# Moving the low halves of 38 weight slabs from VectorE to GpSimd around the norms of a two-layer hybrid backbone

## The chip, the cores and the metric

The kernel runs on one core of a Trainium2 chip. The metric is the device time of one execution in microseconds (us); a kernel's time is the median of its runs. Engines: PE (TensorE, matmul), DVE (VectorE), ACT (ScalarE), POOL (GpSimd), and SP, whose queue issues the DMAs here.

## What is computed

Two layers over 256 context and 256 latent tokens of width 1024. Each layer is a half-step feed-forward, a mixer with three branches on one input projection, and another half-step feed-forward, all between RMS norms:

```python
def ffn_sublayer(x, mod, pre_w, post_w, w_i, w_o):
    shift, scale, gate = mod
    h = modulate(rms_norm(x, pre_w), shift, scale)
    return x + 0.5 * gate * rms_norm(swiglu(h, w_i, w_o), post_w)
...
        u_lat = modulate(rms_norm(h_lat, nw[2]), m_lat[3], m_lat[4])
        p_lat = jnp.split(u_lat @ w_in[l], split_pts, axis=-1)
...
        h_lat = h_lat + m_lat[5] * rms_norm(y_lat, nw[3])
        h_lat = ffn_sublayer(h_lat, m_lat[6:9], nw[4], nw[5], ffn_w_in[l, 1], ffn_w_out[l, 1])
```

The context stream does the same until the second layer's mixer; only the latent stream is returned.

## The kernel before, in words

Activations lie feature-major: 8 tiles of 128 features by 512 tokens (context in columns 0 to 255, stream 0; latents in 256 to 511, stream 1). Every f32 product is made of three matmuls over a high and a low part of each side (`mm3`, lines 206 to 208: high by high, high by low, low by high). A weight slab is 128 x 1024 f32, one DMA of 512 KB. It is split on arrival:

```python
        raw = self.wr_p.tile(shape, F32, name="raw", tag="raw")
        nc.sync.dma_start(raw, src)
        hi = self.wh_p.tile(shape, F32R, name="whi", tag="whi")
        lo = self.wl_p.tile(shape, F32R, name="wlo", tag="wlo")
        nc.scalar.copy(hi, raw)
        (eng or nc.vector).tensor_tensor(lo, raw, hi.bitcast(F32), ALU.subtract)
```

`raw` has 3 buffers, `whi` and `wlo` 4 each. ACT makes `whi` (L200); `wlo = raw - whi` (L201) is DVE's, unless `eng` says otherwise or `self.share` gives every third slab to POOL, as it does during the latent attention and the merge beside it.

Where one sublayer ends and the next begins the two token streams are staggered. `out_phase` runs the last 8 output tiles stream by stream (`by_stream`), and after each stream's tiles calls `norms`: a post-norm of the output `y`, the addition to the residual `h`, the next pre-norm, and its modulation into `uh` and `ul`, the input of the next matmuls. While one stream is in `norms`, PE works on the other. The next sublayer begins the same way: its first tiles (three pairs of feed-forward tiles, `FRONT`, or five projection tiles) also go stream by stream, stream 0 while stream 1 is still in its norms. Call such a place a handoff. There are five: 1, first feed-forward of layer 0 to its projection; 2, output projection of the mixer to the second feed-forward; 3, that to layer 1's first feed-forward; 4, that to layer 1's projection; 5, layer 1's output projection to the last feed-forward, with the latent stream alone.

The links of a norm, by line: ACT squares (`sq`, L280); POOL, for the post-norm, adds seven squares (`sqa`, L284); PE sums them over features (`ssum`, L295); DVE makes the reciprocal root in ten small operations on 128x2 (`rv` L259 to the last `ry` L271, "the root chain"); PE spreads it (`pbc`, L678); then for each of 8 tiles DVE makes `pn` (L329), DVE or POOL adds it to `h` (L330, five of eight on POOL), and after the second root chain DVE makes `u` (L314), ACT `uh` (L316) and DVE `ul` (L317). In handoffs 1, 3 and 4 DVE also adds each output tile to `y` (L502) before it is squared. `pn`, `u` and the `y` addition have one input in PSUM; `ul`, `wlo` and the additions to `h` have both in SBUF.

The order of the instructions on each engine is set by a list scheduler when the program is built; engines run their queues in order.

Of the kernel before, what the change touches and what calls it, by code (L numbers as in the profile page):

```python
# [21 lines left out]
NK = 8  # L22
# [15 lines left out]
NFIRST = 4  # L38
# [95 lines left out]
class K:  # L134
# [56 lines left out]
    def slab(self, src, shape, eng=None):  # L191
        nc = self.nc
        if eng is None and self.share:
            self.nslab += 1
            eng = nc.gpsimd if self.nslab % self.share == 0 else None
# [6 lines that stand above are left out]
        return hi, lo  # L202
# [233 lines left out]
    def ffn(self, l, f, streams=(0, 1), skew=SKEW, ada=(), after=None, start=False):  # L436

        tc, nc = self.tc, self.nc
        n = 0 if f == 0 else 4
        s0 = 0 if f == 0 else 6  # L440
        full = slice(HALF[streams[0]][0], HALF[streams[-1]][1])
        halves = [slice(*HALF[c]) for c in streams]
        split = len(streams) > 1
        with ExitStack() as es:
            ad = es.enter_context(self.pool(name=f"ad{l}{f}", bufs=1))
            pre = self.start(ad, None) if start else None
            if ada and not start:
                self.silu_rows(ad)
            fp = self.fp = es.enter_context(self.pool(name=f"ffn{l}{f}", bufs=1))
            gen = self.ada_gen(ada)  # L450
            due, per = 0.0, (len(ada) * NK + 2) / (60 - (4 if start else 0))

            def step(w):
                nonlocal due
                due += per * w
                while due >= 1:
                    due -= 1
                    next(gen, 0)

            y = [fp.tile([128, T], F32, name=f"y{m}") for m in range(NK)]  # L460
            for g, (f0, f1) in enumerate(FG):
                last = g == len(FG) - 1
                acts = []
                j = f0
                while j < f1:
                    grp = list(range(j, j + (2 if pre and j == 0 else FRONT if j == 0 and split else 1)))
                    at = {jj: (fp.tile([128, T], F32R, name="ah", tag="ah", bufs=10),
                               fp.tile([128, T], F32R, name="al", tag="al", bufs=10)) for jj in grp}
                    slab = lambda jj: [self.slab(self.A["fin"][l, f, jj, q], [128, NK, 128]) for q in range(2)]
                    if pre and j == 0:  # L470
                        for jj in grp:
                            self.ffn_in(full, at[jj], pre[jj], True)
                    elif len(grp) > 1:
                        self.by_stream(grp, streams, slab, lambda jj, c, sl: self.ffn_in(halves[c], at[jj], sl))
                    else:
                        self.ffn_in(full, at[j], slab(j))
                    acts += [at[jj] for jj in grp]
                    j += len(grp)
                    if not (pre and j <= 2):
                        step(2 * len(grp))  # L480
                if last:
                    for _ in gen:
                        pass
                    gain = self.mod_scale(l, s0 + 2, n + 1, 0.0, 0.5, f"fga{l}{f}")
                nk = f1 - f0

                def oslab(m):
                    return self.slab(self.A["fout"][l, f, m][:, f0:f1, :], [128, nk, 128])

                def out_tile(ms, cols, s):  # L490
                    (m,), (s,) = ms, s
                    if not last:
                        step(1)
                    wh, wl = s
                    ps = self.acc.tile([128, T], F32, name="fo", tag="acc")
                    for k in range(nk):
                        ah, al = acts[k]
                        self.mm3(ps[:, cols], wh[:, k, :], wl[:, k, :], ah[:, cols], al[:, cols], k == 0, k == nk - 1)
                    if g == 0:
                        nc.scalar.copy(y[m][:, cols], ps[:, cols])  # L500
                    else:
                        nc.vector.tensor_tensor(y[m][:, cols], y[m][:, cols], ps[:, cols], ALU.add)  # L502

                self.y = y
                self.out_phase(out_tile, oslab, streams, full, skew if last and split else 0, gain if last else None, after)
# [190 lines left out]
    def gdn_pre(self, l, last, ph, pb):  # L696

        nc, A, gp = self.nc, self.A, self.gp
# [16 lines left out]

        nv = max(0, NFIRST - 4)
        vtm = [pb.tile([128, 4, 128], F32, name="vtm", tag="vtm", bufs=4) for _ in range(nv)]
        self.by_stream([21] + list(range(NFIRST)), (0, 1), lambda i: self.win_slab(l, i), half)
        self.mkr = self.dram.tile([64, T], F32, name=f"mkr{l}")
        nc.sync.dma_start(self.mkr, kr[0:64])  # L720
        ps = kr[64:80]
# [39 lines left out]
        for h in range(4):  # L761
            q = ph.tile([128, T - q0], F32, name="qT", tag="qT", bufs=4)
# [909 lines left out]
```

## Time and profile before

| what | value |
|---|---|
| median of 3 runs | 2602.57 us (2599.68 to 2602.64) |
| the profiled execution | 2603.4 us, of which the span of its instructions 2601.6 us |
| PE busy | 2517.8 us (97%) |
| DVE busy | 1763.1 us (68%) |
| ACT busy | 1056.1 us (41%) |
| POOL busy | 261.5 us (10%) |
| mean granted PE clock | 0.981 of full speed |

Busy is time in which an engine executes; a DVE or POOL instruction that has begun and is held up counts as busy, so a mean duration above the shortest ones tells of holding up. The windows view gives busy time and the clock of a stretch, the timeline an engine's instructions in order with the idle time before each in brackets and what ended it.

### The profile page before, as it was taken

The numbers are of one execution on the slowest core, as the hardware profiler recorded it, in microseconds if no ns is written. First come the engines' busy times: TensorE is split into PE (matmuls) and PEld (weight loads), VectorE is DVE, ScalarE is ACT, GpSimd is POOL, SyncE is SP. The second block draws the span as 40 slices with busy tenths as digits, with TensorE's granted clock in tenths as the row PEclk, the third lists the DMA queues.
The fourth block names the chain that finished last, engine by engine and source line by source line (L and its number), as shares of the span: only waits on it lengthen the run. The fifth ranks groups of instructions, "written<-read, shape, count | busy, mean of one in ns | idle before, by whom it ended". The sixth has DMA issues, their size and how long they took to land.

```text
span 2601.6 us, 42990 instructions
## 1 busy us (share of the span) xinstructions
PE 2517.8 (97%) x17034; PEld 2202.6 (85%) x17034; DVE 1763.1 (68%) x3364; ACT 1056.1 (41%) x1742; POOL 261.5 (10%) x248
## 2 busy tenths in 40 slices
PE   7999999999999999999999999999999899998998
PEld 5888888888888877998888898888989798788998
DVE  6778668674787454685665687767678678755554
ACT  3432235545444343553222443223465444554543
POOL 0000012012100012400000200000302110023001
PEclk9999999999999999999999999999999899998999
DMA  7556543234232331565444456555334325334653
GB/s 266 179 194 197 170 142 123 98 107 133 74 135 87 110 104 57 170 195 169 151 142 144 140 169 201 177 174 162 115 108 125 124 91 199 122 114 139 189 185 122
DMA packets 121561, 377.37 MB, mean 145 GB/s; under 512 B 14736, under 2 KB 24208, under 8 KB 121360
## 3 DMA queue, kind: packets, MB, share of 16 engines
q1 hardware_dynamic: 121360, 374.63, 45.2%
q8 instruction: 134, 2.20, 0.3%
q14 instruction: 67, 0.55, 0.1%
HBM read 352.69 MB, written 21.89 MB: 144 GB/s over the span
## 4 chain that ended last, share of the span: by engine, by line
PE 85%; DVE 7%; ACT 3%; issue 2%; DMA 2%; POOL 1%; SPq 0%; POOLq 0%; ACTq 0%; DVEq 0%
PE fgu L206 11%; PE fgu L208 11%; PE fgu L207 11%; PE pj L206 7%; PE pj L208 7%; PE pj L207 7%; PE fo L207 5%; PE fo L208 5%; PE fo L206 5%; DVE wlo L201 1%; PE pbc L678 1%; PE ssum L295 1%; PE br L206 1%; PE br L207 1%; PE br L208 1%
## 5 line engine op out<-in xcount | busy, mean ns | idle before, releaser
L200 ACT CAST whi<-raw 128x1024 fp32r<-128x1024 f32 (+1 forms) x486 | 500.9, 1032 | 977.9 <-issue 305.1
L201 DVE TENSOR_TENSOR wlo<-raw,whi 128x1024 fp32r<-128x1024 f32 (+1 forms) x460 | 559.3, 1217 | 267.9 <-ACT whi L200 259.7
L206 PE MATMUL fgu<-uh,whi 128*128 128x512 f32 (+1 forms) x1504 | 529.6, 354 | 2.7 <-ACT uh L316 2.2
L207 PE MATMUL fgu<-ul,whi 128*128 128x512 f32 (+1 forms) x1504 | 529.7, 353 | 0.1
L208 PE MATMUL fgu<-uh,wlo 128*128 128x512 f32 (+1 forms) x1504 | 529.5, 353 | 0.2 <-DVE wlo L201 0.2
L206 PE MATMUL pj<-uh,whi 128*128 128x512 f32 (+1 forms) x1072 | 381.3, 357 | 8.6 <-ACT whi L200 4.4
L208 PE MATMUL pj<-uh,wlo 128*128 128x512 f32 (+1 forms) x1072 | 375.5, 353 | 1.9 <-POOL wlo L201 1.2
L207 PE MATMUL pj<-ul,whi 128*128 128x512 f32 (+1 forms) x1072 | 376.2, 352 | 0.0
L231 DVE CUSTOM_DVE_ANT_0 junk<-wa,cb,bada 128x1024 f32<-128x1024 f32 x268 | 343.5, 1282 | 11.6 <-DMA wa<-in_ada 7.0
L206 PEld LDWEIGHTS fgu<-uh,whi 128*128 128x128 f32 x1504 | 286.5, 191 | 41.7 <-ACT uh L316 3.1
L208 PEld LDWEIGHTS fgu<-uh,wlo 128*128 128x128 f32 x1504 | 286.6, 191 | 38.6 <-DVE wlo L201 1.0
L207 PEld LDWEIGHTS fgu<-ul,whi 128*128 128x128 f32 x1504 | 286.7, 191 | 37.9 <-DVE ul L317 0.5
L207 PE MATMUL fo<-al,whi 128*128 128x256 f32 (+1 forms) x896 | 291.4, 325 | 0.5 <-DVE al L434 0.3
L208 PE MATMUL fo<-ah,wlo 128*128 128x256 f32 (+1 forms) x896 | 290.6, 325 | 0.0
L206 PE MATMUL fo<-ah,whi 128*128 128x256 f32 (+1 forms) x896 | 290.5, 325 | 0.0
L206 PEld LDWEIGHTS pj<-uh,whi 128*128 128x128 f32 x1072 | 208.9, 195 | 31.5 <-ACT whi L200 4.7
L208 PEld LDWEIGHTS pj<-uh,wlo 128*128 128x128 f32 x1072 | 208.5, 195 | 25.2 <-POOL wlo L201 1.9
L207 PEld LDWEIGHTS pj<-ul,whi 128*128 128x128 f32 x1072 | 209.2, 195 | 21.0 <-DVE ul L317 0.4
L284 POOL TENSOR_TENSOR sqa<-sqa,sq 128x256 f32<-128x256 f32 x60 | 63.5, 1058 | 1297.7 <-ACT sq L280 1295.9
L207 PEld LDWEIGHTS fo<-al,whi 128*128 128x128 f32 x896 | 168.7, 188 | 17.0 <-DVE al L434 1.6
L206 PEld LDWEIGHTS fo<-ah,whi 128*128 128x128 f32 x896 | 168.5, 188 | 15.3
L208 PEld LDWEIGHTS fo<-ah,wlo 128*128 128x128 f32 x896 | 168.5, 188 | 15.3
(368 smaller groups left out, 3497.5 us busy)
## 6 DMA issues: line engine op xcount, KB each, us to landing
raw<-in_fin SPq DMA_DIRECT2D x184, 512.0 KB, 3.5
wa<-in_ada SPq DMA_DIRECT2D x136, 512.0 KB, 4.1
raw<-in_win SPq DMA_DIRECT2D x128, 512.0 KB, 3.5
raw<-in_fout SPq DMA_DIRECT2D x79, 512.0 KB, 3.6
raw<-in_fout SPq DMA_DIRECT2D x32, 384.0 KB, 3.2
raw<-in_wb SPq DMA_DIRECT2D x24, 512.0 KB, 3.6
raw<-in_wo SPq DMA_DIRECT2D x21, 512.0 KB, 3.8
ws<-in_ada SPq DMA_DIRECT2D x8, 512.0 KB, 7.9
```

Of the source, the lines that this page charges most:

```text
L200: nc.scalar.copy(hi, raw)
L201: (eng or nc.vector).tensor_tensor(lo, raw, hi.bitcast(F32), ALU.subtract)
L206: nc.tensor.matmul(out, wh, xh, start=start, stop=False)
L207: nc.tensor.matmul(out, wh, xl, start=False, stop=False)
L208: nc.tensor.matmul(out, wl, xh, start=False, stop=stop)
L231: op = nc.vector.tensor_tensor_reduce(out=self.junk, in0=w, in1=self.cb[:, t], scale=1.0, scalar=self.bada[:, l, i, m:m + 1], op0=ALU.mult ...
L284: eng.tensor_tensor(S["acc"], S["acc"], sq, ALU.add)
L295: nc.tensor.matmul(S["ps"][:, i:i + 1], a[:, i * 128:(i + 1) * 128], self.ones[:, 0:1], start=S["first"], stop=(m == NK - 1 and a is S["pa ...
L678: self.nc.tensor.transpose(pb[:, c * 128:(c + 1) * 128], y[:, c:c + 1].to_broadcast([128, 128]), self.ident)
```

## The change

`slab` gets an engine at two places: POOL for the first three pairs of feed-forward tiles where there are two streams, for the first two tiles of the last feed-forward, and for the five projection tiles that go stream by stream. Slabs that are loaded a second time for stream 1 are included: 7 slabs in handoffs 1 and 4, 10 in handoffs 2 and 3, 4 in handoff 5, 38 in all. The slabs of the output tiles in the same handoffs stay on DVE.

```diff
@@ -466,7 +466,9 @@
+
+                    eng = nc.gpsimd if len(grp) > 1 or (f == 1 and not split and j < 2) else None
-                    slab = lambda jj: [self.slab(self.A["fin"][l, f, jj, q], [128, NK, 128]) for q in range(2)]
+                    slab = lambda jj: [self.slab(self.A["fin"][l, f, jj, q], [128, NK, 128], eng) for q in range(2)]
@@ -715,7 +717,8 @@
-        self.by_stream([21] + list(range(NFIRST)), (0, 1), lambda i: self.win_slab(l, i), half)
+
+        self.by_stream([21] + list(range(NFIRST)), (0, 1), lambda i: self.win_slab(l, i, nc.gpsimd), half)
```

The scheduler then orders the queues anew. Line numbers from L467 on are 2 or 3 higher in the changed kernel.

POOL's queue in handoff 1, from the square sums of stream 1's output to its last addition to the residual, before:

```order
L284 TENSOR_TENSOR sqa<-sqa,sq 128x256 x6
L330 TENSOR_TENSOR h_103<-h_103,pn 128x256
L330 TENSOR_TENSOR h_104<-h_104,pn 128x256
L330 TENSOR_TENSOR h_106<-h_106,pn 128x256
L330 TENSOR_TENSOR h_107<-h_107,pn 128x256
L330 TENSOR_TENSOR h_109<-h_109,pn 128x256
```

and in the changed kernel:

```order
L284 TENSOR_TENSOR sqa<-sqa,sq 128x256 x4
L201 TENSOR_TENSOR wlo<-raw,whi 128x1024 x4
L284 TENSOR_TENSOR sqa<-sqa,sq 128x256 x2
L201 TENSOR_TENSOR wlo<-raw,whi 128x1024
L330 TENSOR_TENSOR h_103<-h_103,pn 128x256
L330 TENSOR_TENSOR h_104<-h_104,pn 128x256
L201 TENSOR_TENSOR wlo<-raw,whi 128x1024
L330 TENSOR_TENSOR h_106<-h_106,pn 128x256
L330 TENSOR_TENSOR h_107<-h_107,pn 128x256
L330 TENSOR_TENSOR h_109<-h_109,pn 128x256
```

Four slabs now stand ahead of the last two square sums, one ahead of the additions to `h` and one among them. Handoffs 3 and 4 read the same at this place; in handoff 2 it is two, then three, and five behind the additions.

DVE's queue in handoff 1 at the root chain of the norm that these square sums feed, before:

```order
L502 TENSOR_TENSOR y_609<-y_609,fo 128x256
L201 TENSOR_TENSOR wlo<-raw,whi 128x1024
L259 TENSOR_SCALAR rv<-ssum 128x2
L201 TENSOR_TENSOR wlo<-raw,whi 128x1024
L262 TENSOR_SCALAR rt<-rv 128x2
L201 TENSOR_TENSOR wlo<-raw,whi 128x1024
L263 TENSOR_SCALAR ry<-rt 128x2
```

and in the changed kernel:

```order
L504 TENSOR_TENSOR y_609<-y_609,fo 128x256
L259 TENSOR_SCALAR rv<-ssum 128x2
L262 TENSOR_SCALAR rt<-rv 128x2
L263 TENSOR_SCALAR ry<-rt 128x2
L265 TENSOR_TENSOR rt<-ry 128x2
```

Three slabs have left DVE here, two of them from inside the chain.

POOL's queue in handoff 5, before:

```order
L284 TENSOR_TENSOR sqa<-sqa,sq 128x256 x6
L330 TENSOR_TENSOR h_22933<-h_22933,pn 128x256
L330 TENSOR_TENSOR h_22934<-h_22934,pn 128x256
L330 TENSOR_TENSOR h_22936<-h_22936,pn 128x256
L330 TENSOR_TENSOR h_22937<-h_22937,pn 128x256
L330 TENSOR_TENSOR h_22939<-h_22939,pn 128x256
```

and in the changed kernel:

```order
L284 TENSOR_TENSOR sqa<-sqa,sq 128x256 x4
L201 TENSOR_TENSOR wlo<-raw,whi 128x1024
L284 TENSOR_TENSOR sqa<-sqa,sq 128x256
L201 TENSOR_TENSOR wlo<-raw,whi 128x1024 x2
L284 TENSOR_TENSOR sqa<-sqa,sq 128x256
L201 TENSOR_TENSOR wlo<-raw,whi 128x1024
L330 TENSOR_TENSOR h_22933<-h_22933,pn 128x256
```

The sixth square sum now stands behind three slabs, and a fourth runs next to the root chain. PE's queue is the same as before in handoff 5.

## Rows read from the trace of the kernel before

**Rows 1.** The page, part 1: busy time, share of the span, instructions.

```profile
PE 2517.8 (97%) x17034; PEld 2202.6 (85%) x17034; DVE 1763.1 (68%) x3364; ACT 1056.1 (41%) x1742; POOL 261.5 (10%) x248
```

**Rows 2.** Windows, one row per handoff: width, busy time of each engine, PEclk, DMA.

```profile
375.00:455.00 80.00, 73.89 (x576) 72.47 (x575) 59.57 (x148) 37.79 (x75) 22.11 (x23) 0.94 0.35 115
1050.00:1150.00 100.00, 97.81 (x781) 95.33 (x780) 73.52 (x145) 58.65 (x112) 29.62 (x32) 1.00 0.55 179
1420.00:1510.00 90.00, 85.09 (x628) 81.60 (x627) 59.99 (x133) 40.49 (x69) 20.86 (x22) 0.96 0.43 135
1835.00:1910.00 75.00, 68.49 (x520) 67.11 (x519) 56.42 (x144) 36.02 (x72) 18.97 (x20) 0.91 0.30 93
2340.00:2410.00 70.00, 59.26 (x437) 57.67 (x436) 40.81 (x82) 34.03 (x61) 21.60 (x22) 0.85 0.45 142
```

**Rows 3.** Groups by line and form: `wlo` on DVE and on POOL.

```profile
L201 DVE TENSOR_TENSOR wlo<-raw,whi 128x1024 fp32r<-128x1024 f32 x424 | 524.9, 1239 | 254.6 <-ACT whi L200 246.6 <-PE br L208 0.3
L201 POOL TENSOR_TENSOR wlo<-raw,whi 128x1024 fp32r<-128x1024 f32 x24 | 59.5, 2483 | 468.7 <-ACT whi L200 447.7 <-ACT spl L625 10.6 <-PE mqp L208 10.2
```

**Rows 4.** Timeline, DVE, three stretches: start, duration, line, operation.

```profile
426.56 0.47 DVE L329 SCALAR_TENSOR_TENSOR pn<-y,fga,pbc 128x256 f32<-128x256 f32 x1
...
1995.30 2.25 DVE L266 TENSOR_TENSOR rt<-rt,rv 128x2 f32<-128x2 f32 x1
...
2013.71 2.59 DVE L820 TENSOR_TENSOR X<-X,ip 128x255 f32<-128x255 f32 x1
2016.34 2.59 DVE L818 TENSOR_TENSOR ip<-Lt,X 128x256 f32<-128x256 f32 x1
```

**Rows 5.** Timeline, POOL, the same stretches.

```profile
426.38 1.54 POOL L330 TENSOR_TENSOR h<-h,pn 128x256 f32<-128x256 f32 x2 [0.29 <-DVE pn L329]
...
1995.12 2.40 POOL L201 TENSOR_TENSOR wlo<-raw,whi 128x1024 fp32r<-128x1024 f32 x1
...
2016.24 2.40 POOL L201 TENSOR_TENSOR wlo<-raw,whi 128x1024 fp32r<-128x1024 f32 x1 [0.22 <-ACT whi L200]
```

**Rows 6.** Timeline, DVE, handoff 1.

```profile
404.63 1.23 DVE L201 TENSOR_TENSOR wlo<-raw,whi 128x1024 fp32r<-128x1024 f32 x1
...
406.95 0.87 DVE L317 SCALAR_TENSOR_TENSOR ul<-u,mod,uh 128x256 fp32r<-128x256 f32 x2
...
410.96 1.27 DVE L317 SCALAR_TENSOR_TENSOR ul<-u,mod,uh 128x256 fp32r<-128x256 f32 x3
412.14 1.07 DVE L502 TENSOR_TENSOR y<-y,fo 128x256 f32<-128x256 f32 x3
...
417.77 1.22 DVE L201 TENSOR_TENSOR wlo<-raw,whi 128x1024 fp32r<-128x1024 f32 x1
```

**Rows 7.** Timeline, ACT, handoff 1: the casts of the projection's first three slabs.

```profile
404.37 1.05 ACT L200 CAST whi<-raw 128x1024 fp32r<-128x1024 f32 x1 [0.73 <-DMA raw<-in_win]
...
407.10 1.03 ACT L200 CAST whi<-raw 128x1024 fp32r<-128x1024 f32 x1
...
409.33 1.05 ACT L200 CAST whi<-raw 128x1024 fp32r<-128x1024 f32 x1
```

**Rows 8.** Timeline, POOL, handoff 1.

```profile
413.21 2.52 POOL L284 TENSOR_TENSOR sqa<-sqa,sq 128x256 f32<-128x256 f32 x2 [8.70 <-ACT sq L280]
```

**Rows 9.** Timeline, PE, handoff 1.

```profile
415.79 1.44 PE L295 MATMUL ssum<-ones,sqa 128*128 128x1 f32 x6 [2.27 <-POOL sqa L284]
```

**Rows 10.** Timeline, ACT, handoff 5.

```profile
2372.21 1.05 ACT L200 CAST whi<-raw 128x1024 fp32r<-128x1024 f32 x1 [2.03 <-DMA raw<-in_fin]
...
2373.96 1.99 ACT L200 CAST whi<-raw 128x1024 fp32r<-128x1024 f32 x2
...
2376.31 0.42 ACT L280 ACTIVATE sq<-yo 128x256 f32<-128x256 f32 x1
```

**Rows 11.** Timeline, DVE, handoff 5: first and last operation of the root chain (ten).

```profile
2380.35 0.16 DVE L259 TENSOR_SCALAR rv<-ssum 128x2 f32<-128x2 f32 x1 [0.17 <-PE ssum L295]
...
2382.12 0.16 DVE L271 SCALAR_TENSOR_TENSOR ry<-rt,ry 128x2 f32<-128x2 f32 x1
```

## Prediction, on record before the run

> **What bounds the kernel now.** I read the page's busy times first: PE is busy 2517.8 of 2601.6 us [rows 1], so 83.8 us of PE idleness, and what a lowered clock costs, is all that a change off PE can win. Next I asked the windows view for the five handoffs, since all 38 moved slabs lie there. Width less PE busy is 6.1, 2.2, 4.9, 6.5 and 10.7 us of idleness, 30.4 us together [rows 2]. PE's granted clock is 1.00 in the handoff with 2.2 us of idleness and 0.94, 0.96, 0.91, 0.85 in the others; width times what is missing gives 4.8 + 3.6 + 6.8 + 10.5 = 25.7 us of full-speed time lost to it [rows 2]. So the most that could be won is 30 + 26 us; what can be lost has no such end. Third, the timeline of handoff 1, where the longest wait is one of 2.27 us: `ssum` waits for POOL's last two square sums [rows 9], which wait for squares of `y` [rows 8], whose additions stand on DVE behind the last `ul` [rows 6]. DVE is what ends last there, and it is busy 59.6 of 80 us in that handoff [rows 2].
>
> **What is removed.** 38 instructions of 1.24 us from DVE, 47 us, at the cost of 38 of 2.48 us on POOL, 94 us [rows 3]. ACT's casts, the DMAs and all matmuls stay. In handoff 1 the two slabs that stood inside the root chain (1.22 us each [rows 6]) go, and PE, whose queue is ordered anew, now has 22 ready projection matmuls ahead of the awaited `ssum` instead of 6. At 97.81 us for 781 [rows 2] one is 0.125 us, so 16 more are 2.0 us of cover.
>
> **What is added: a hold-up of DVE.** While POOL ran a slab from 1995.12 to 1997.52 [rows 5], a root-chain operation with two SBUF inputs, 0.16 us long elsewhere [rows 11], took 2.25 us [rows 4]. With two slabs back to back, the second from 2016.24 to 2018.64 [rows 5], DVE got one operation through per slab, each 2.59 us [rows 4]. An operation with an input in PSUM is not held: `pn` took 0.47 us while POOL was adding to `h` [rows 4, 5]. So `ul`, the root chain and the additions to `h` wait behind a slab on POOL for up to 2.4 us, while `u`, `pn` and the `y` additions do not. A slab that left DVE saves 1.2 us; one that meets such an operation on POOL costs up to 2.25.
> The Trainium skill's page "SBUF — State Buffer", section "SBUF: two separate sides", says that these two engines take a shared port pair as an exclusive lock for a whole instruction, and that DVE needs it with two SBUF inputs; the rows above agree. By that rule taken to its end, with a waiting DVE operation behind all 38 slabs, the change would cost an estimated 38 times (2.40 - 1.22) = 45 us; by the rows only the slabs that overlap a chain count, and I count those.
>
> **Handoffs 1, 3 and 4** (the same queue on POOL at this place). The first three slabs are cast by 405.42, 408.13 and 410.38 [rows 7]. POOL can start the first when DVE's own slab lets go at 405.86 [rows 6]. From there to the last `ul` the port must carry three slabs, 7.2 us, and eight `ul`. Two `ul` in a row take 0.87 us [rows 6], and because starts overlap I take 0.40 each: 3.2 us. So 405.86 + 10.4 = 416.3 against 412.2 [rows 6], 4.1 us later. The `y` additions follow, then squares and POOL's last two square sums. Before, those ended 3.6 us after the `y` additions began (412.14 to 415.73 [rows 6, 8]), of which about 1.0 us was POOL held by DVE's slab; that goes, but the fourth slab may stand ahead, 0 to 2.4 us. The `ssum` comes 3.1 to 5.5 us later. The 2.0 us of cover leaves 1.1 to 3.5, middle 2.3. Later in the same norm one slab meets the end of the root chain (0 to 2.25 us, against two slabs of 1.2 us removed from a chain that PE's queued matmuls mostly hide: 0), and one among POOL's additions to `h` holds those and DVE's back by 0 to 2.4 us, of which I keep 1.5. The last root chain loses one DVE slab, a gain of 1.2 us at most. I take 2.3 + 1.5 - 0.8 = 3 us each (0 to 6), 9 us for the three. Handoff 3 has four reloaded slabs behind this, beside `ul` of stream 1; matmuls of stream 0 cover them and I take nothing, with up to 2 us if that cover ends early.
>
> **Handoff 2.** Only two slabs stand ahead of the last square sums, but three in a row stand between them and the additions to `h`, where the handoffs above have one, so two more can meet the root chain: 2 times (2.25 - 1.2) = 2.1 us above the 3 us. PE has almost no idleness here to soak up a delay [rows 2]. I take 5 us (0 to 8).
>
> **Handoff 5.** PE's queue is unchanged and DVE's four slabs are over before the chain (`rv` waits for `ssum` alone [rows 11]), so nothing is won. POOL's queue can be walked. First slab: cast ends 2373.26 [rows 10], slab to 2375.7. Fifth square sum, taken as 0.77 us like an addition of the same size [rows 5], to 2376.4. Second and third slab, both cast by 2375.95 [rows 10], to 2381.2. Sixth square sum, whose square was there at 2376.73 [rows 10], to 2382.0. I allow 0.7 us from there to `rv` for `ssum` and the handing over: 2382.7, against 2380.35 [rows 11], 2.4 us later. The fourth slab holds the port from 2382.0 to 2384.4; `rv` reads PSUM and passes, the nine behind it wait, then go at 0.2 us: 2386.2, against 2382.28 [rows 11]. PE has nothing else to do, so 4 us (2.4 without the hold-up).
>
> **The sum.** 9 + 5 + 4 = 18 us, and 2 us for the clock, which has been lower wherever PE idled 4.9 us or more [rows 2]: handoff 2 would now idle that long, and 4 percent of some 50 us is the like of what the others lose. The profiled execution took 2603.4 us, 0.8 above the median of 2602.57, so 2603.4 + 20 - 0.8 = 2622.6; I say 2622.
>
> **Rivals.**
> *DVE's relief decides: faster.* The mechanism is the root chain and `ul` in handoffs 1, 3 and 4: five DVE slabs of 1.2 us leave each norm of stream 1. If POOL's slabs mostly run beside `u`, `pn` and the `y` additions, which they don't hold, the `ssum` comes 1 us sooner three times, the last chain 1.2 us sooner three times, and of the 15.2 us lost to the clock there [rows 2] about half returns: -3 - 3.6 - 7.6, against +2.4 in handoff 5. That is -12 us, 2591. It decides if the mean hold-up of a DVE operation by a slab is under about 1 us. For it: half of DVE's operations in these chains have an input in PSUM. Against: eight `ul` in a row with casts that come in time for POOL to be there [rows 6, 7], and the two rows of 2.59 us [rows 4].
> *Cover hides both: no change.* The projection matmuls that PE now holds ready absorb a delayed norm, and only handoff 5 shows: +2.4 to 4, 2605. For it: 2.0 us of new cover in handoffs 1, 3 and 4. Against: PE already waited there before [rows 9], so a delay has no slack to use up.
> *The clock goes too.* Each delay above lengthens a stretch in which PE idles, and in the four handoffs with long idleness 3.6 to 10.5 us went to the clock [rows 2]. If each handoff loses 4 us more so, 20 us on top of the 18: 2641. Idle stretches that merely shift cost nothing more, which is why it is not the forecast.
>
> **How the numbers follow.** Forecast 0.60; faster 0.10; no change 0.15; the clock too 0.15. A measurement of this kernel tells about 0.2%, 5.2 us, from no change, so "within" is 2597.4 to 2607.8. The low ends of the terms (0, 0, 2.4) fall into the case of no change, so the range runs from 2603, inside that case, to 2640, just short of the last; it leaves out the faster case, part of the unchanged and the upper part of the last, 2 in 10. Chances: faster 0.10, within 0.15, slower 0.75.
>
> **What would show it.** Right: POOL's `wlo` at about 2.4 us in the handoffs with `ul` or root-chain operations of 1 to 2.4 us beside them; the `ssum` of handoff 1 waiting longer than 2.27 us or coming 3 to 5 us later; in handoff 5 the first root chain 4 us later; DVE's busy time falling by well under 47 us, since held operations count as busy. Wrong: `ul` at 0.4 to 0.5 us beside POOL's slabs; PE idleness and clock in the five windows unchanged or better; a span under 2597.

## The result, and the profile after

The changed kernel takes 2648.82 us (median of 4 runs, 2639.19 to 2652.28) against 2602.61 us for the kernel before: a ratio of 1.0168, 95% interval 1.0157 to 1.018. It is 46 us slower. I had forecast 2622, so the sign was right, and the range (2603 to 2640) ended 9 us too low.

The profiled execution took 2647.33 us with a span of 2645.6, 44.0 more than before. Page, part 1, of the changed kernel; it answers to [rows 1]:

```profile
PE 2535.9 (96%) x17034; PEld 2216.8 (84%) x17034; DVE 1774.9 (67%) x3326; ACT 1056.5 (40%) x1742; POOL 347.4 (13%) x286
```

This line alone splits the loss. PE does the same 17034 matmuls, yet is busy 18.1 us longer (2517.8 before): the same work at a lower clock. The mean granted clock says so in every execution on record: 0.980 to 0.984 in the kernel before, 0.971 to 0.974 in the changed one. The other 25.9 us of the 44.0 are idleness, 109.7 against 83.8. DVE lost 38 instructions of 1.24 us, 47 us of work, and is busy 11.8 us *longer*.

The windows view of the changed kernel, one row per handoff, answers to [rows 2]. Each window runs from the same piece of the program to the same piece as there, to a whole us.

```profile
375.00:464.00 89.00, 78.72 (x565) 76.07 (x564) 62.46 (x137) 36.59 (x75) 38.18 (x30) 0.87 0.32 101
1059.00:1172.00 113.00, 102.19 (x777) 99.13 (x776) 75.15 (x134) 58.52 (x112) 53.04 (x42) 0.95 0.50 157
1442.00:1544.00 102.00, 91.37 (x627) 86.35 (x626) 66.06 (x129) 40.55 (x70) 39.74 (x30) 0.90 0.40 125
1869.00:1951.00 82.00, 72.38 (x528) 70.05 (x527) 60.69 (x136) 35.84 (x72) 34.92 (x28) 0.88 0.27 87
2380.00:2454.00 74.00, 59.56 (x434) 57.67 (x434) 35.40 (x78) 33.75 (x61) 28.76 (x25) 0.84 0.43 134
```

Against the widths and PE busy times of [rows 2], in us:

| handoff | predicted, clock apart | wider by | of it PE idle | of it PE busy (the clock) |
|---|---|---|---|---|
| 1 | 3 | 9 | 4.2 | 4.8 |
| 2 | 5 | 13 | 8.6 | 4.4 |
| 3 | 3 | 12 | 5.7 | 6.3 |
| 4 | 3 | 7 | 3.1 | 3.9 |
| 5 | 4 | 4 | 3.7 | 0.3 |
| sum | 18, and 2 for the clock | 45 | 25.3 | 19.7 |

The whole loss lies in the five handoffs. What I called the clock's 2 us is 18 to 20. The windows' counts of matmuls differ by up to 11 from those of before, some 1.4 us of PE, so the split of one handoff's loss is rough.

**Handoff 1, DVE**, timeline of the changed kernel, answering to [rows 6]:

```profile
406.31 4.84 DVE L317 SCALAR_TENSOR_TENSOR ul<-u,mod,uh 128x256 fp32r<-128x256 f32 x2 [0.50 <-ACT uh L316]
...
411.86 1.27 DVE L317 SCALAR_TENSOR_TENSOR ul<-u,mod,uh 128x256 fp32r<-128x256 f32 x3
...
414.22 4.81 DVE L317 SCALAR_TENSOR_TENSOR ul<-u,mod,uh 128x256 fp32r<-128x256 f32 x3
...
425.27 2.21 DVE L271 SCALAR_TENSOR_TENSOR ry<-rt,ry 128x2 f32<-128x2 f32 x1
```

**The same stretch on POOL**:

```profile
405.94 4.92 POOL L201 TENSOR_TENSOR wlo<-raw,whi 128x1024 fp32r<-128x1024 f32 x2 [0.71 <-ACT whi L200]
413.50 4.85 POOL L201 TENSOR_TENSOR wlo<-raw,whi 128x1024 fp32r<-128x1024 f32 x2 [2.63 <-ACT whi L200]
420.01 1.53 POOL L284 TENSOR_TENSOR sqa<-sqa,sq 128x256 f32<-128x256 f32 x2 [1.66 <-ACT sq L280]
425.08 2.38 POOL L201 TENSOR_TENSOR wlo<-raw,whi 128x1024 fp32r<-128x1024 f32 x1 [3.55 <-ACT whi L200]
```

Two `ul` took 0.87 us before; beside two slabs on POOL they take 4.84. Between the slabs (411.86) three take the usual 1.27. The last `ul` ends at 419.03 where it ended at 412.23, and even the tenth operation of the root chain, at 425.27, waits out a slab.

**And on PE**, where only the three longest waits are shown:

```profile
416.20 0.39 PE L207 MATMUL pj<-ul,whi 128*128 128x256 f32 x1 [1.70 <-DVE ul L317]
...
418.69 0.58 PE L207 MATMUL pj<-ul,whi 128*128 128x256 f32 x1 [1.86 <-DVE ul L317]
...
421.59 1.87 PE L295 MATMUL ssum<-ones,sqa 128*128 128x1 f32 x8 [1.90 <-POOL sqa L284]
```

The one wait of 2.27 us [rows 9] has become three in a row, with three matmuls between one and the next. Handoffs 3 and 4 show the same three (1.70, 1.87, 1.90 and 1.72, 1.87, 1.89 us). What follows is the clock's part. In the changed kernel the clock stands at the lower of its two levels, 1.2 GHz, around these waits (417 to 427), comes back to the upper one, 2.4 GHz, for seven us, and falls again behind one more wait, of 1.01 us. Windows of that second fall, of the kernel before and then of the changed one, with the seven us ahead of it:

```profile
434.00:448.00 14.00, 12.35 (x96) 11.90 (x95) 11.49 (x34) 6.56 (x15) 3.62 (x2) 0.95 0.23 75
```

```profile
427.00:434.00 7.00, 5.48 (x44) 5.08 (x43) 6.17 (x11) 2.41 (x6) 5.44 (x6) 0.98 0.54 187
434.00:448.00 14.00, 13.96 (x66) 13.96 (x67) 5.42 (x21) 4.04 (x11) 2.21 (x3) 0.51 0.40 134
```

From 434 on PE is busy 13.96 of 14.00 us and gets 66 matmuls done where 96 went through before: it stands at the lower level though it has work all the time. PE's waiting has ended by then; this part of the price is paid behind it. Handoffs 3 and 4 show the same two falls, the second behind a wait of 0.7 us.

**Handoff 2.** DVE's second root chain of the changed kernel, then POOL and PE:

```profile
1137.03 1.90 DVE L262 TENSOR_SCALAR rt<-rv 128x2 int32<-128x2 int32 x1
1138.96 2.27 DVE L263 TENSOR_SCALAR ry<-rt 128x2 int32<-128x2 int32 x1
1141.26 2.25 DVE L265 TENSOR_TENSOR rt<-ry 128x2 f32<-128x2 f32 x1
```

```profile
1136.49 7.01 POOL L201 TENSOR_TENSOR wlo<-raw,whi 128x1024 fp32r<-128x1024 f32 x3 [2.89 <-ACT whi L200]
```

```profile
1145.05 0.66 PE L680 MATMUL pbc<-ident,ry 128*128 128x128 f32 x2 [5.96 <-DVE ry L271]
```

Three slabs in a row let one operation of the chain through each, and PE waits 5.96 us where it did not wait before.

**The waits view** groups all of this; PE's rows in the changed kernel (us in total, times, longest):

```profile
PE pbc L680 <- DVE ry L271: 21.0, 14, 6.0
PE ssum L295 <- POOL sqa L284: 12.9, 5, 4.9
...
PE pj L207 <- DVE ul L317: 7.7, 5, 1.9
...
PE fgu L207 <- DVE ul L317: 3.6, 2, 1.9
```

The same view of the kernel before:

```profile
PE pbc L678 <- DVE ry L271: 12.6, 8, 2.4
...
PE ssum L295 <- POOL sqa L284: 7.5, 4, 2.3
```

That is 8.4 us more for the root chains, 5.4 for POOL's square sums and 11.3 new ones for `ul`: 25.1, all but 0.8 of the new idleness. That POOL makes each slab later than DVE did brings PE no wait of its own: its waits for a `wlo` of POOL's are 1.2 us in both kernels.

### The profile page after: what moved, and what is told of

Same layout as the page of the kernel before. It is cut to its first block, busy times and chain, and to the rows that moved or that the text cites. A ratio compares the mean times of both kernels' runs of the same rounds, so it can differ in the third digit from the quotient of the medians.

```text
span 2645.6 us, 43015 instructions
## 1 busy us (share of the span) xinstructions
PE 2535.9 (96%) x17034; PEld 2216.8 (84%) x17034; DVE 1774.9 (67%) x3326; ACT 1056.5 (40%) x1742; POOL 347.4 (13%) x286
## 5 line engine op out<-in xcount | busy, mean ns | idle before, releaser
L201 DVE TENSOR_TENSOR wlo<-raw,whi 128x1024 fp32r<-128x1024 f32 (+1 forms) x422 | 513.0, 1216 | 254.7 <-ACT whi L200 246.2
L201 POOL TENSOR_TENSOR wlo<-raw,whi 128x1024 fp32r<-128x1024 f32 (+1 forms) x64 | 153.3, 2402 | 553.0 <-ACT whi L200 539.8
```

## Experiments

My theory after the result: POOL's slabs hold DVE's `ul` and root-chain operations, PE waits for those, and PE's waits bring the clock down. The rivals: POOL's queue (square sums and additions to `h` come late behind slower slabs, DVE is not held); each moved slab costs alike wherever it stands; the clock falls for a reason of its own.

### What on POOL holds what on DVE

Three kernels, built on the kernel before: DVE keeps its 38 slabs, and POOL gets extra work behind each, on a scratch tile that nothing reads: the first, the second or the last two of the added lines.

```diff
         (eng or nc.vector).tensor_tensor(lo, raw, hi.bitcast(F32), ALU.subtract)
+        nc.gpsimd.tensor_tensor(self.scr, hi.bitcast(F32), hi.bitcast(F32), ALU.subtract)
+        nc.gpsimd.tensor_copy(self.scr, hi.bitcast(F32))
+        nc.gpsimd.tensor_copy(self.scr[:, 0, 0:1], hi[:, 0, 0:1].bitcast(F32))
+        nc.gpsimd.memset(self.scr, 0.0); nc.gpsimd.memset(self.scr, 0.0); nc.gpsimd.memset(self.scr[:, 0:4], 0.0)
```

> The kernel before, in which DVE keeps its 38 slabs and GpSimd gets, behind each of them, one subtraction of the same 128x1024 size with both inputs from SBUF, into a scratch tile that nothing reads. Theory (a GpSimd instruction that reads SBUF holds up DVE's instructions whose inputs all lie in SBUF, for as long as it runs): slower by at least the 46 us of the change, 2645 to 2690, since DVE's own slabs are held up too. Rival (GpSimd's queue: the square sums and the additions to h come late because they stand behind slower slabs; DVE itself is not held): 15 to 30 us, 2617 to 2633, as in the other two kernels of this set. Rival (only two inputs on GpSimd's side hold): as the theory here, but not for the copy.

> As the kernel with the extra subtractions, every engine's order the same, but GpSimd's extra instruction is a copy: one input from SBUF, 128x1024, about as long (2.4 us, from 1.2 us for 512 columns). Theory (any GpSimd instruction that reads SBUF holds DVE up): as with the subtraction, within 10 us of it. Rival (queue alone): 2617 to 2633. Rival (only two inputs hold): 2603 to 2620.

> As the kernel with the extra subtractions, but GpSimd's extra work is a copy of one column, to fix the place, and three memsets of the scratch tile (1024, 1024 and 512 columns, 0.95 us per 1024 by the profile of before, so 2.4 us together): it reads no SBUF. GpSimd's queue is as full as with the subtraction. Theory (what reads SBUF holds): 2603 to 2615, DVE's instructions beside the memsets of their usual length. Rival (queue): the same as with the subtraction, whatever that is. Rival (any GpSimd instruction holds): as with the subtraction.

Measured: 2652.61 us with the subtraction (ratio 1.0195, 1.018 to 1.0211), 2628.7 with the copy (1.0103, 1.0088 to 1.0118), 2618.96 with the memsets (1.0067, 1.0052 to 1.0082). The subtraction lies in my theory's range. The copy lies below it, in the range that I had given the rival of the queue, and the memsets lie 4 us above theirs, so the times alone don't settle it. POOL's extra groups by line and form, in that order, without the copy of one column; these durations take in what DVE holds up on POOL, and the copy, 1.04 us at its shortest, is shorter than the 2.4 us that I had estimated:

```profile
L203 POOL TENSOR_TENSOR scr<-whi 128x1024 f32<-128x1024 f32 x38 | 87.6, 2305 | 28.7 <-ACT whi L200 23.1 <-PE ssum L297 3.5
```

```profile
L203 POOL COPY scr<-whi 128x1024 f32<-128x1024 f32 x38 | 54.6, 1438 | 29.2 <-ACT whi L200 24.3 <-PE ssum L297 3.5
```

```profile
L205 POOL MEMSET scr<- 128x1024 f32 x38 | 36.3, 955 | 2.0
L204 POOL MEMSET scr<- 128x1024 f32 x38 | 36.2, 953 | 2.1
L206 POOL MEMSET scr<- 128x512 f32 x38 | 20.0, 526 | 2.1
```

The three fill POOL's queue with 87.6, 54.6 and 92.5 us, and the fullest queue costs least. The second root chain of handoff 2 on DVE, beside the subtraction (POOL runs eight of them from 1131.04 to 1149.65):

```profile
1134.18 1.73 DVE L267 TENSOR_TENSOR rt<-ry 128x2 f32<-128x2 f32 x1
```

beside the copies:

```profile
1126.82 0.88 DVE L267 TENSOR_TENSOR rt<-ry 128x2 f32<-128x2 f32 x1
```

and beside the memsets, with POOL's own rows in a second fence:

```profile
1127.74 0.58 DVE L267 TENSOR_SCALAR rt<-rv 128x2 int32<-128x2 int32 x1
1128.36 0.55 DVE L268 TENSOR_SCALAR ry<-rt 128x2 int32<-128x2 int32 x1
1128.94 0.16 DVE L270 TENSOR_TENSOR rt<-ry 128x2 f32<-128x2 f32 x1
...
1129.21 1.22 DVE L201 TENSOR_TENSOR wlo<-raw,whi 128x1024 fp32r<-128x1024 f32 x1
```

```profile
1127.35 0.95 POOL L205 MEMSET scr<- 128x1024 f32 x1
1128.36 0.52 POOL L206 MEMSET scr<- 128x512 f32 x1
...
1129.21 0.95 POOL L204 MEMSET scr<- 128x1024 f32 x1
```

A two-input DVE operation waits out what is left of the subtraction (1.73) and of the shorter copy (0.88), and passes the memset at its usual 0.16; DVE's own slab at 1129.21 starts with a memset and takes its usual 1.22. I counted all DVE instructions that came up while one of these POOL instructions (of at least 0.9 us) still had 0.3 us or more to go. With all inputs in SBUF, 32 of 32 were held by the subtraction, 22 of 22 by the copy, and none of 42 two-input ones by the memset. With an input in PSUM none was held by any of them, 48 in all. The one exception shows in the rows: the chain's two operations with a single SBUF input *are* held by a memset (0.58 and 0.55, each until the memset beside it ends).

The Trainium skill's page "SBUF — State Buffer", section "SBUF: two separate sides", says just this: a DVE instruction with two SBUF inputs needs the shared ports only against a GpSimd instruction that reads SBUF, one in a two-port mode against any GpSimd instruction. These rows agree on the first half. The two held operations with one input fit the second, but in which mode they ran no row shows.

What it costs: the scratch tile's memory came free late, so the extra work ran in rows of up to eight behind the additions to `h`, and in handoffs 1 and 4 it also kept the cast tiles long enough for PE to wait 7.17 us for a cast. I therefore read only handoffs 2, 3 and 5, by the distance between two same DVE or ACT instructions around each: they grow by 12.1, 13.7 and 5.1 us with the subtraction, 5.8, 6.6 and 0.8 with the copy, 1.1, 2.6 and 1.6 with the memset. That is 30.9, 13.2 and 5.3 us. A queue as full, in which POOL reads almost nothing, costs 5 of the 31; most of the rest goes with the hold-up. That tells of slabs behind the additions to `h`. For those ahead of the square sums the changed kernel's own trace decides: in handoffs 1, 3 and 4 POOL stands idle for 1.66 us ahead of the last two square sums (420.01 above) and in handoff 2 for 2.36 us ahead of the last one, waiting for ACT's squares. So POOL's queue isn't what makes them late there; in handoffs 1, 3 and 4 the held `ul` is, behind which the additions to `y` stand on DVE. In handoff 5 alone does the last square sum stand straight behind slabs.

### The same slabs in pieces

```diff
-        (eng or nc.vector).tensor_tensor(lo, raw, hi.bitcast(F32), ALU.subtract)
+        for p in range(parts):      # 4 for the 38 slabs, else 1
+            cut = slice(p * s, (p + 1) * s)
+            (eng or nc.vector).tensor_tensor(lo[:, cut], raw[:, cut], hi[:, cut].bitcast(F32), ALU.subtract)
```

> The changed kernel with each of the 38 GpSimd slabs written as four subtractions of 128x256 in place of one of 128x1024. By the additions to h one takes 0.8 us, so a slab 3.2 us in place of 2.4. Theory (held for the length of one instruction): a held DVE instruction waits at most 0.8 us, and as many DVE instructions get through as there are pieces, so chains shorten although GpSimd takes longer: 2622 to 2645. Rival (the slab's own lateness or GpSimd's queue): 38 slabs 0.8 us later each, 2650 to 2670.

Measured 2640.08 (1.0148, 1.0131 to 1.0165): inside the theory's range, near its end. A piece takes 0.78 us, so POOL spends 3.1 us per slab in place of 2.4, and still the time falls by 9. The longest `ul` falls from 2.60 to 0.97 us. Handoff 1 grows by 4.2 us in place of 9.3, but handoff 2 by 14.5: a chain of ten short operations meets one piece after another there, so that POOL's whole time counts.

### Which slabs

```diff
                     if i not in sl:
+                        self.again = c != streams[0]
                         sl[i] = slab_fn(i)
...
-... self.win_slab(l, i, nc.gpsimd), half)
+... self.win_slab(l, i, nc.gpsimd if not self.again else None), half)
```

The feed-forward's slabs are chosen alike (handoff 5's four count with the first stream), and the second kernel turns the condition round.

> The changed kernel with the 12 reloaded slabs (2, 4, 4 and 2 of handoffs 1 to 4) back on DVE: 26 slabs on GpSimd, those loaded for stream 0 and the four of handoff 5. Theory (slabs that meet `ul`, the last square sums and a root chain are what costs): handoffs 1, 3, 4 and 5 nearly as in the changed kernel, handoff 2 cheaper by some 4 us since two of the three slabs in a row on its root chain are reloaded ones: 2636 to 2646. Rival (every slab costs alike, 46/38 = 1.2 us): 2634 with nothing gained in any one place. Rival (GpSimd's total load): the same 2634.

> The changed kernel with only the 12 reloaded slabs on GpSimd. Theory: two of them meet a root chain in handoff 2 (4 us), one meets an addition to `h` in each of handoffs 1, 3 and 4 (1 to 2 us each): 2606 to 2613, and no wait of PE for `ul`. Rival (each slab costs alike): 12 times 1.2 us, 2617. My prediction took nothing for them in handoff 3: 2603 to 2606 if they are free everywhere.

Measured 2632.07 (1.0114, 1.0097 to 1.0131) and 2611.01 (1.0034, 1.0021 to 1.0048): 29.7 us for 26 slabs, 8.7 for 12. That is 1.1 and 0.7 us each, but with the intervals 1.0 to 1.3 and 0.5 to 1.0, so the totals alone don't show that they cost differently. reloaded_only lies in my range, first_stream_only below mine; the rival's single number there, 2634, was nearer. By place the rival fails: the reloaded slabs alone cost 0.1, 1.6, 2.9 and 0.1 us in handoffs 1 to 4, the others 2.2, 11.3, 10.1, 1.5 and 3.5 in the five. The two sums make 38.4, and together the slabs cost 46: handoffs 1 and 4 lose 9 and 7 us with both kinds, and at most 2.2 with either. There a reloaded slab falls among the additions to `h` (POOL at 430.54, DVE's addition beside it 2.47 us) just behind a held root chain, and the longest half-clock stretch of handoff 1, 13.7 us, does not occur with either kind alone.

### Square sums off POOL

```diff
-... slice(*HALF[c]), i, self.nc.vector if i == NK - 1 else self.nc.gpsimd)
+... slice(*HALF[c]), i, self.nc.vector)
```

> The changed kernel with all square sums of the output phases on DVE (25 or so additions of 128x256 move from GpSimd to DVE), so that none stands behind a slab in GpSimd's queue. Rival (GpSimd's queue is what costs): PE's waits for GpSimd's square sums, 12.9 us in five places, go, and with them some of the clock: 2625 to 2638. Theory (hold-up of DVE): these additions have two SBUF inputs and are held on DVE by the same slabs: 2643 to 2660, and DVE's square sums beside slabs take about 2 us.

Measured 2653.73 (1.0197, 1.0181 to 1.0214), 5 us slower than the change, as the theory had it. The rival was half right: PE's idleness falls from 109.7 to 102.7 us. But PE's busy time rises from 2535.9 to 2547.5, the clock's part again. What DVE takes over is held there too: six of the square sums take over 0.25 us more than usual, up to 2.57 us.

### PE's waits filled

The changed kernel, with six more matmuls ahead of each one that reads `ul` in the first slab of a handoff, into the unused half of the same PSUM tile. The square sums' matmuls were tied behind them, so that PE's order in handoffs 1, 3 and 4 stays that of the changed kernel.

```diff
         nc.tensor.matmul(out, wh, xh, start=start, stop=False)
+        for _ in range(self.nfill):     # 6 in the first slab of stream 0, handoffs 1 to 4
+            nc.tensor.matmul(self.spare, wh, xh, start=False, stop=False)
         nc.tensor.matmul(out, wh, xl, start=False, stop=False)
```

> The changed kernel with 192 more matmuls on PE and no other work: in each of handoffs 1 to 4, 6 ahead of each of the 8 matmuls that read `ul` in the first projection or feed-forward slab of stream 0. They repeat the matmul before them into PSUM columns that nothing reads; they stand where PE waits for a held `ul`, and cost 0.125 us each at full clock, 6 us per handoff. In the changed kernel PE waits 6.5, 2.3, 5.9 and 5.5 us there, and half-clock stretches of 24, 10, 20 and 20 us follow. Theory (PE's waits lower the clock, and that is 18 of the 46 us): the half-clock stretches of handoffs 1, 3 and 4 shrink by more than half, and although 24 us of matmuls are added the time falls to 2630 to 2645. Rival (the clock falls for another reason, and waits are all that counts): stretches as before, PE's added matmuls beyond its waits are paid, 2652 to 2665.

Measured 2637.32 (1.0137, 1.0122 to 1.0153). PE does 192 matmuls more, about 24 us of them, and the kernel is 11.5 us *faster* than the change. Its profiled execution is the fastest of its four (2633.71 us), but the mean granted clock is back in all of them, 0.979 to 0.981. Page, part 1, and the windows of handoffs 1, 3 and 4:

```profile
PE 2541.7 (97%) x17226; PEld 2225.7 (85%) x17226; DVE 1769.7 (67%) x3326; ACT 1056.8 (40%) x1742; POOL 350.6 (13%) x286
```

```profile
374.40:457.00 82.60, 77.04 (x613) 75.23 (x612) 60.46 (x138) 36.14 (x73) 38.93 (x30) 0.96 0.34 111
...
1437.50:1535.40 97.90, 89.84 (x679) 85.75 (x678) 67.23 (x132) 41.06 (x71) 39.34 (x30) 0.99 0.43 135
1860.40:1942.30 81.90, 75.64 (x574) 74.05 (x572) 58.38 (x135) 35.92 (x72) 35.03 (x27) 0.92 0.28 86
```

In handoff 1 the three waits are now two, with the filler in them:

```profile
418.89 0.39 PE L212 MATMUL pj<-ul,whi 128*128 128x256 f32 x1 [0.60 <-DVE ul L324]
...
421.79 1.05 PE L301 MATMUL ssum<-ones,sqa 128*128 128x1 f32 x8 [1.57 <-POOL sqa L289]
```

Less an estimated 24 us of filler, PE is busy 2517.7 us, as in the kernel before. The granted clock is 0.96, 0.99 and 0.92 where the change had 0.87, 0.90 and 0.88. POOL still holds `ul` (14 times, for 24.6 us in all, against 15 times and 27.1), and DVE, ACT and POOL run the same instructions in the same order there. So the rival falls: in these handoffs nothing but PE's waits and what fills them was altered, and the clock came back, from 24 and 20 us at half clock to 7 and 3 in handoffs 1 and 3. In handoff 4, where a wait of 2.14 us for `ry` is left, it came back by less than the half that I had expected (20 us to 14), and the handoff takes as long as in the change. Handoff 2, where the filler does not stand at the wait, got worse, 15.6 us in place of 13.6.

Two readings on record limit this. Not every wait is paid twice: in the kernel with the copies PE idles 22.0 us more than in the kernel before (105.8 against 83.8), and its busy time is the same, 2517.6 us.

```profile
PE 2517.6 (96%) x17034; PEld 2202.3 (84%) x17034; DVE 1778.6 (68%) x3364; ACT 1057.3 (40%) x1742; POOL 313.5 (12%) x286
```

And not every fall stands behind a wait. In handoff 1 of the kernel before, PE was busy for ten us, with the one-column matmuls of the second norm's sums among the others, and the clock fell all the same:

```profile
422.00:432.00 10.00, 10.00 (x89) 10.00 (x88) 6.36 (x14) 5.99 (x13) 4.82 (x6) 1.00 0.73 262
432.00:436.00 4.00, 4.00 (x24) 4.00 (x23) 2.93 (x10) 0.06 (x1) 0.00 (x0) 0.57 0.75 260
```

So filling the waits gives the clock back here; which waits cost it, and what else does, stays open.

### The same filler in the kernel before

18 such matmuls ahead of the awaited `ssum` of handoffs 1, 3 and 4 (nine in each of the first two steps of the slab), and in a second kernel 82 more in handoff 5.

> The kernel before (no slab moved) with 18 more matmuls of 0.125 us in each of handoffs 1, 3 and 4, which repeat a matmul of the first slab into PSUM columns that nothing reads, ahead of the square-sum matmuls for which PE waits 2.3 us there: as long as the wait. Half-clock stretches of 10, 7 and 14 us lie in these handoffs now (and one of 3 us behind the first). Theory (waits lower the clock): some of these 31 to 34 us go, each for half its length, and the filler hides in the wait: 2588 to 2600, below both kernels. Rival (waits alone count): 2602 to 2608.

> As the kernel before with filled waits, and in handoff 5, where PE has nothing else to do, 82 more matmuls behind the square-sum matmuls of the two norms (16 in each root chain, 6 to 8 between the sums). 20.5 us at half clock lie there now, 5.8 us of them under feed-forward matmuls. Theory: the clock stays up through the chain, 3 us less at the feed-forward's start and up to 2 us less in the chain's own sums and broadcasts: 3 to 5 us below the run with handoffs 1, 3 and 4 alone. Rival: the fillers get in the way of the sums behind them, no gain or up to 3 us more.

Measured 2598.58 (0.9986, 0.9977 to 0.9995) and 2604.45 (1.0005, 0.9993 to 1.0016). The first is the fastest kernel of this study, 3.8 us below the kernel before; half-clock stretches ahead of the kernel's last 12 us shrink from 92 to 72 us. The second came out 5.9 us above the first, further than even the rival's 3. In handoff 5 half-clock time falls only from 20.5 to 17.1 us, and the handoff takes 6.8 us longer. The two kernels do the same in handoff 1, yet one's trace has 6.8 us at half clock there and the other's none: the clock of a single handoff differs that much between two executions.

## Why the prediction was right, and where it was wrong

*The hold-up of DVE*, price and rule: right. `ul`, root-chain operations and additions to `h` take up to 2.6, 2.4 and 2.5 us beside a slab, operations with an input in PSUM are not held. Added up over DVE's instructions that take over 0.25 us more than the median of the same operation and shape, held time is 35 us before and 90 after, 27 of it `ul`.

*Handoffs 1, 3 and 4*, 3 us each without the clock: measured 4.2, 5.7 and 3.1 of idleness, inside 0 to 6. The number held, but two of its steps failed, and what made up for them is not shown. I had the fourth slab perhaps ahead of the square sums, and three ahead of the last `ul`; it was four, and the last `ul` came 6.8 us later in place of 4.1. And the 2.0 us of cover, "22 ready projection matmuls ahead of the awaited `ssum`", was none: those matmuls read `ul`. They waited for the same held instructions, in two waits of 1.70 and 1.86 us. The `ssum` began 5.8 us later (421.59 against 415.79), just beyond my 3.1 to 5.5.

*Handoff 2*, 5 us: 8.6 of idleness, just above its 0 to 8. I priced two held operations in the root chain at 2.1 us above the others; three met it, for 6.4 us in all, and PE had nothing to cover them.

*Handoff 5*, 4 us: measured 4, by another route. POOL's queue went as walked: the sixth square sum ends at 2422.68, 1.0 later than worked out (2382.0, and this piece of program runs 39.7 us later than before). But the fourth slab ends just as the chain begins, and holds nothing. PE instead, at half clock, takes the eight matmuls for the sums in one go of 1.87 us. PE, then POOL, of the changed kernel, and the chain's first and last operation, which answer to [rows 11]:

```profile
2422.74 1.87 PE L295 MATMUL ssum<-ones,sqa 128*128 128x1 f32 x8 [4.95 <-POOL sqa L284]
```

```profile
2421.94 0.74 POOL L284 TENSOR_TENSOR sqa<-sqa,sq 128x256 f32<-128x256 f32 x1
2422.62 2.37 POOL L201 TENSOR_TENSOR wlo<-raw,whi 128x1024 fp32r<-128x1024 f32 x1
```

```profile
2424.64 0.16 DVE L259 TENSOR_SCALAR rv<-ssum 128x2 f32<-128x2 f32 x1 [13.58 <-PE ssum L295]
...
2426.43 0.16 DVE L271 SCALAR_TENSOR_TENSOR ry<-rt,ry 128x2 f32<-128x2 f32 x1
```

*The clock*, 2 us: this is the step on which the forecast failed. It measured 18.1 us in PE's busy time, and in the trace of the filled kernel, less the filler, none of it is left. I had read in [rows 2] that the clock was lower wherever PE idled 4.9 us or more, and concluded that only handoff 2 would join them. I treated it as a state that a handoff is in or not, where in these handoffs it was an amount that grew: three waits in place of one went with two stretches of 10 us and more at half clock in handoffs 1, 3 and 4, where there had been two or three of 3 to 7 us. My rival "the clock goes too" had this size almost exactly, 20 us, which is 4 in each of five handoffs, and 2641; I held it down to 0.15 on the ground that idle stretches that merely shift cost nothing. They did not shift, they multiplied: PE waits seven times for `ul`, 11.3 us in all, where it never did before. Of the 26 us between my 20 and the measured 46, the clock is 16 to 18; the rest is idleness, mostly in handoffs 2 and 3.

*The other rivals.* "DVE's relief decides" fell with DVE's busy time going up. "Cover hides both" fell with the cover that waits for `ul`. The estimate from the rule taken to its end, 45 us and 2648, hits the time, but not by its route: it would have had DVE's busy time rise by 45 us, which rose by 11.8, and the 12 reloaded slabs cost 0.7 us each. The rule says what holds what; the price was what PE waited for, 25 us, and the clock, 18.

## What to carry to other kernels

Work that goes from DVE to GpSimd is not off DVE's path as long as it reads SBUF: ask which DVE instructions with SBUF inputs come up beside it, and put it beside those with an input in PSUM. Before counting queued work as cover for a wait, look at what that work itself reads. And price new PE waits twice, once for their length and once for the half-clock stretches that may follow, which can be longer than the waits: here 18 us on 25, while 22 us of other idleness, in the kernel with the copies, added nothing to PE's busy time. Matmuls that do nothing, about as long as the wait, can be cheaper than idling.

## What the runs showed that I had not expected

Around and behind three waits of 1.7 to 1.9 us the clock stood at the lower level for two stretches of over 10 us, at the upper one for seven us between them, and from 434 to 448 PE was busy 13.96 of 14.00 us: having work did not bring the clock back within that stretch.

A single-input copy of 128x1024 takes POOL 1.04 us at its shortest where the two-input subtraction of that size takes 1.89 (1.44 and 2.31 on average, with what DVE holds up), and it holds DVE just as surely, only for less long.

A memset on POOL, which reads nothing, still holds DVE's operations with one SBUF input (0.58 and 0.55 us in place of 0.16 to 0.17).
